# Experts' weights in loads of 1 MB with 8 KB rows, and sorted rows by one indirect gather per two experts

## The chip, the cores and the metric

The kernel runs on one core of one Trainium2 chip. The metric is the time of one execution on the device, in microseconds (us). A program of the framework gives each engine its own queue of instructions, which it works through in order: TensorE (PE; PEld is its weight load), VectorE (DVE), ScalarE (ACT), GpSimd (POOL) and SyncE (SP). SP computes nothing; it issues DMA transfers, which 16 DMA engines move. GpSimd issues the indirect transfers, whose row numbers lie in SBUF.

## The reference, cut to what matters

The model has two layers of a first network, each a mixer followed by a mixture of experts, and then two layers of a second network with a context of its own. The experts are what the change touches:

```python
def hier_moe(h, w_group, b_group, w_expert, b_expert, w1, w3, w2):   # 512 tokens, D = 1024
    ...
    g_val, g_idx = lax.top_k(g_prob, 1)                              # one of 4 groups
    ...
    e_val, e_idx = lax.top_k(jax.nn.softmax(e_logits, axis=-1), MOE_TOP_K)   # 2 of its 8 experts
    ...
    hid = jax.nn.silu(jnp.einsum('td,edf->tef', t, w1)) * jnp.einsum('td,edf->tef', t, w3)
    hid = hid * combine.astype(hid.dtype)[:, :, None]
    y = jnp.einsum('tef,efd->td', hid, w2)                           # 32 experts, width 128
```

512 tokens with two experts each are 1024 pairs of token and expert, on average 32 for each of 32 experts.

## The kernel before

`moe` (L727) runs once in each of the two layers of the first network. It normalizes the tokens, computes the router, counts the pairs of each expert and gives each pair a place so that pairs of one expert lie in consecutive rows. Eight indirect scatters (L872, four tiles of 128 tokens, two experts each) write the tokens' rows into `dxs` in HBM in that order. At the end eight indirect gathers (L1008) bring the experts' results back from `dys` in the tokens' order.

In between a loop (L961) runs over 16 pairs of experts q, and over a 17th step for one overflow block. An expert gets 64 rows (CAP); an expert with more has the rest in overflow blocks, of which the first is the 17th step and others would run in a loop of the device that is skipped when there are none. In step q:

- `fetch_rows` (L885) loads the sorted rows of the two experts of pair q + 2: two DMAs of SP, each 64 rows of 4 KB into 64 partitions of `xr`, starting at a place that SP reads from SBUF into a register. What belongs to the next expert comes along.
- `fetch` (L767) loads the weights of pair q + 2 by `load` (L762): four loads of the first layer's weights `w13` (two 128-row parts of D each, for both experts) and two of the second layer's `w2`, 512 KB each, in tiles of 4 KB in each of 128 partitions. The pool has WBUFS = 13 such tiles.
- `columns` (L894) transposes rows on TensorE (`px`), `hidden` (L908) multiplies with `w13` (`pa`), `turn` (L925) transposes the hidden values (`ph`), and `results` (L933) multiplies with `w2` (`py`) and scatters the result rows into `dys` by an indirect DMA on GpSimd, which leaves out rows that are not the expert's own: `blocks` (L1039) gives those a row number beyond 4096 in `rows`.
- `self.fill` (L980, L1817) mixes in steps of other work: projections of the context (`ctx_pair`, L1909). Each step loads 512 KB into a tile `stage` (L286), splits it into a high and a low part on ScalarE (`whi`, L278) and VectorE (`wlo`, L279), and multiplies (`mm`, L304). After two steps ScalarE writes `out` (L1361) and SP stores it into `dpc` (L1936). In layer 0 there are 0.7 such steps to a pair, in layer 1 one.

The framework orders each engine's instructions by a model of its own before the kernel runs; the order in the trace is the one that it found. SP's queue holds the weight loads, the row loads, the stage loads and the stores.

Of the kernel before, what the change touches and what calls it, by code (L numbers as in the profile page):

```python
# [104 lines left out]
def layout(inp):  # L105
# [54 lines left out]
    A["w13"] = w13.reshape(2, 16, 2, 4, 2, P, 256).transpose(0, 1, 3, 5, 2, 4, 6).reshape(2, 16, 4, P, 2, 512)  # L160
    A["w2"] = g["moe_w2"].reshape(2, 16, 2, P, D)
# [40 lines left out]
WBUFS = 13  # L202
# [51 lines left out]
class K:  # L254
# [472 lines left out]
    def moe(self, l, fills, tail=None, norm=False):  # L727
# [8 lines left out]
        with ExitStack() as es:  # L736
# [7 lines left out]
            dxs, dys = self.pdram.tile([D + C, D], FT, name=f"dxs{l}"), self.pdram.tile([D, D], FT, name=f"dys{l}")  # L744
            zero = pht.tile([P, D], FT, tag="ht", name=self.n("zero"))
            nc.gpsimd.memset(zero[0:C, :], 0.0)
            nc.sync.dma_start(dxs[D:, :], zero[0:C, :])
# [14 lines left out]
            def load(src):  # L762
                w = pq.tile([P, D], FT, tag="w", name=self.n("w"))
                nc.sync.dma_start(w.rearrange("p (a f) -> p a f", a=src.shape[1]) if len(src.shape) == 3 else w, src)
                return w

            def fetch(q):  # L767

                return ([load(I["w13"][l, q, kk].rearrange("p t f -> p (t f)")) for kk in range(4)],
                        [load(I["w2"][l, q, t]) for t in range(2)])  # L770
# [137 lines left out]
            def hidden(x, ws, n):  # L908

                pa = self.ps("a", "pa")  # L910
                m = KT // len(ws)
                for b, w in enumerate(ws):
                    for k in range(b * m, b * m + m):
                        for t in range(n):
                            c = t * 512 + (k - b * m) * 256
                            nc.tensor.matmul(pa[t * C:(t + 1) * C, :256], x[:, k, t * C:(t + 1) * C], w[:, c:c + 256],  # L916
                                             start=(k == 0), stop=(k == KT - 1))
# [15 lines left out]
            def results(w2, h, row):  # L933

                n = len(w2)
                r = slice(0, n * C)
                yr = pt.tile([P, D], FT, tag="yrow", name=self.n("yrow"), bufs=2)
                for b in range(2):
                    py = self.ps("mm", "py")
                    for t in range(n):  # L940
                        nc.tensor.matmul(py[t * C:(t + 1) * C, :], h[:, t * C:(t + 1) * C], w2[t][:, b * S:(b + 1) * S], start=True, stop=True)
# [6 lines left out]
            def slot(s):  # L948

                xr = fetch_rows([slots[0:1, 2, s]])  # L950
# [3 lines left out]
                ws = [load(I["w13"][l, ds(e[0], 1), b * 2:b * 2 + 2, :, ds(e[1], 1), :].rearrange("o a p u f -> (o p) (a u) f")) for b in range(2)]  # L954
                return xr, (ws, [load(I["w2"][l, ds(e[0], 1), ds(e[1], 1)].rearrange("o u p f -> (o u p) f"))])

            place = lambda q: [offi[0:1, 2 * q + t:2 * q + t + 1] for t in range(2)]
            xr = [fetch_rows(place(q)) for q in range(AHEAD)]
            prev, wrote, owed = None, [], 0.0
            x_ = columns(xr[0], 2)  # L960
            for q in range(17):  # L961
                if q + AHEAD < 16:
                    xr.append(fetch_rows(place(q + AHEAD)))
                    weights.append(fetch(q + AHEAD))
                elif q + AHEAD == 16:
                    a, b = slot(slice(0, 1))
                    xr.append(a)
                    weights.append(b)
# [1242 lines left out]
```

## Time and profile before

| | |
|---|---|
| time, median of three runs | 3120.87 us (3116.51 to 3122.72) |
| the profiled execution | 3123.15 us |
| its span, first to last instruction | 3121.4 us |
| mean granted TensorE clock, share of 2.4 GHz | 0.958 |
| busy share of the span: TensorE, VectorE, ScalarE, GpSimd | 92%, 61%, 40%, 15% |
| moved by DMA | 513.22 MB |
| weight loads of experts (L764) | 198 of 512 KB |
| row loads of experts (L891) | 66 of 256 KB |

A busy TensorE is not at its peak: its matmuls overlap, and at half the clock (1.2 GHz) it is as busy and half as fast. The granted clock in a stretch is given as a share of 2.4 GHz. The experts' loops lie at 334 to 546 us (layer 0) and 1174 to 1427 us (layer 1) of the span.

### The profile page before, as it was taken

How to read it: one execution, taken by the hardware profiler on the slowest of the kernel's cores; microseconds unless marked ns; L12 is line 12 of the kernel's file. 1: busy time of each engine (PE TensorE's matmuls, PEld its weight loads, DVE VectorE, ACT ScalarE, POOL GpSimd, SP SyncE). 2: the span in 40 equal slices, each digit the busy share in tenths (PEclk: the TensorE clock that was granted, in tenths of full speed). 3: DMA queues.
4: the chain of work that ended last, by engine and by line, in shares of the span. 5: the costliest groups of instructions: out<-in, count | busy, mean ns of one | idle time of the engine just before them, and what ended most of it. 6: DMA issues, size and time to landing. Idle time of an engine off the chain costs nothing.

```text
span 3121.4 us, 39028 instructions
## 1 busy us (share of the span) xinstructions
PE 2871.6 (92%) x14382; PEld 2198.0 (70%) x14382; DVE 1904.4 (61%) x3188; ACT 1258.4 (40%) x1989; POOL 470.5 (15%) x413
## 2 busy tenths in 40 slices
PE   7998877799999998778789999999999999999998
PEld 5566655677777785556677667777788776777887
DVE  7786312688889861115879954448745985453434
ACT  4444212456535452114653444334434344433434
POOL 0121000223313220001320000012111000001212
PEclk9998988899999999889999999999999999999999
DMA  8678988655542288786562222235644222222332
GB/s 302 208 249 291 338 291 303 220 156 170 162 150 64 87 292 303 267 292 201 164 211 89 64 62 86 67 96 177 201 128 147 84 66 68 78 93 76 95 95 81
DMA packets 177331, 513.22 MB, mean 164 GB/s; under 512 B 22768, under 2 KB 42864, under 8 KB 177136
## 3 DMA queue, kind: packets, MB, share of 16 engines
q1 hardware_dynamic: 167760, 485.51, 48.2%
q0 software_dynamic: 9376, 25.18, 2.2%
q8 instruction: 114, 1.87, 0.2%
q14 instruction: 81, 0.66, 0.1%
HBM read 472.98 MB, written 46.53 MB: 166 GB/s over the span
## 4 chain that ended last, share of the span: by engine, by line
PE 44%; DVE 4%; issue 1%; ACT 1%; DMA 1%; POOL 0%; DVEq 0%; ACTq 0%; POOLq 0%
PE mm L304 35%; PE po L1497 1%; PE pp L1494 1%; DVE wlo L279 1%; PE po L1420 1%; PE st L1409 1%; PE as L1710 1%; DMA stage<-in_modT_dram 1%; DVE stage L340 1%; PE as L1717 0%; PE pv L1606 0%; PE pv L1607 0%; PE pv L1605 0%; PE po L1431 0%; DVE junk L340 0%
## 5 line engine op out<-in xcount | busy, mean ns | idle before, releaser
L304 PE MATMUL mm<-hhi,whi 128*128 128x512 f32 (+1 forms) x2488 | 951.0, 383 | 61.1 <-ACT whi L278 52.7
L304 PE MATMUL mm<-hhi,wlo 128*128 128x512 f32 (+1 forms) x2488 | 931.9, 375 | 20.1 <-DVE wlo L279 19.7
L304 PE MATMUL mm<-hlo,whi 128*128 128x512 f32 (+1 forms) x2488 | 927.4, 373 | 1.5 <-POOL hlo L396 1.3
L279 DVE TENSOR_TENSOR wlo<-stage,whi 128x1024 fp32r<-128x1024 f32 (+2 forms) x477 | 547.0, 1149 | 458.6 <-issue 189.2
L278 ACT ACTIVATE whi<-stage 128x1024 fp32r<-128x1024 f32 (+2 forms) x477 | 461.3, 968 | 880.6 <-PE mm L304 586.5
L304 PEld LDWEIGHTS mm<-hhi,whi 128*128 128x128 f32 x2488 | 492.2, 198 | 157.6 <-ACT whi L278 58.5
L304 PEld LDWEIGHTS mm<-hhi,wlo 128*128 128x128 f32 x2488 | 492.0, 198 | 113.1 <-DVE wlo L279 31.8
L304 PEld LDWEIGHTS mm<-hlo,whi 128*128 128x128 f32 x2488 | 492.9, 198 | 85.1 <-issue 16.6
L340 DVE SCALAR_TENSOR_TENSOR stage<-stage,row 128x1024 f32<-128x1024 f32 x160 | 211.8, 1333 | 24.2 <-DMA stage<-in_adaT_dram 15.7
L1622 DVE SCALAR_TENSOR_TENSOR cv<-cfu,cols,cv 128x512 f32<-128x512 f32 x240 | 171.5, 756 | 1.3
L1586 POOL TENSOR_TENSOR merged<-sig,merged 128x512 f32<-128x512 f32 x48 | 83.7, 1744 | 560.2 <-DVE sig L1585 551.0
L304 PE MATMUL mm<-brh,whi 128*128 128x512 f32 (+1 forms) x384 | 142.4, 371 | 13.5 <-DVE merged L1583 5.8
L304 PE MATMUL mm<-brh,wlo 128*128 128x512 f32 (+1 forms) x384 | 141.8, 372 | 12.9 <-DVE wlo L279 12.6
L304 PE MATMUL mm<-brl,whi 128*128 128x512 f32 (+1 forms) x384 | 139.0, 362 | 0.1
L916 PE MATMUL pa<-w,xc 128*64 128x256 f32 x1056 | 126.3, 381 | 0.2 <-issue 0.2
L903 DVE COPY xc<-px 128x512 f32<-128x512 f32 (+1 forms) x34 | 23.0, 675 | 157.8 <-PE px L900 157.8
L916 PEld LDWEIGHTS pa<-w,xc 128*64 128x64 f32 x1056 | 77.7, 138 | 52.8 <-issue 17.7
L943 POOL DMA_INDIRECT dys<-yrow,ri x32 | 32.1, 1004 | 469.9 <-DVE yrow L1102 449.8
L304 PEld LDWEIGHTS mm<-brh,whi 128*128 128x128 f32 x384 | 74.6, 194 | 29.2 <-DVE merged L1583 6.6
L304 PEld LDWEIGHTS mm<-brh,wlo 128*128 128x128 f32 x384 | 74.2, 194 | 28.5 <-DVE wlo L279 16.7
L1361 ACT ACTIVATE att<-as,stat 128x512 f32<-128x512 f32 (+2 forms) x80 | 54.7, 687 | 69.6 <-DVE stat L1472 66.0
L304 PEld LDWEIGHTS mm<-brl,whi 128*128 128x128 f32 x384 | 74.9, 195 | 9.7 <-issue 0.5
(474 smaller groups left out, 4283.4 us busy)
## 6 DMA issues: line engine op xcount, KB each, us to landing
stage<-in_winA_dram SPq DMA_DIRECT2D x252, 512.0 KB
w<-in_w_dram SPq DMA_DIRECT2D x198, 512.0 KB
stage<-in_adaT_dram SPq DMA_DIRECT2D x96, 512.0 KB
stage<-in_modT_dram SPq DMA_DIRECT2D x64, 512.0 KB
stage<-in_ssmA_dram SPq DMA_DIRECT2D x49, 512.0 KB
stage<-in_wbrA_dram SPq DMA_DIRECT2D x96, 256.0 KB
xr<-dxs SPq DMA_DIRECT2D x66, 256.0 KB
stage<-in_woutA_dram SPq DMA_DIRECT2D x24, 512.0 KB
```

The lines of the kernel that those rows point to most:

```text
L278: self.nc.scalar.activation(hi, src, AF.Copy)
L279: self.nc.vector.tensor_tensor(lo, src, hi.bitcast(FT), op=OP.subtract)
L304: nc.tensor.matmul(ps[:, po:po + n], w[:, k * P:(k + 1) * P], h[:, so:so + n], start=(k == first and w is hi and h is hh), stop=(k == last ...
L340: self.nc.vector.scalar_tensor_tensor(t if out is None else out, t, 1.0, vec, op0=OP.mult, op1=OP.mult, accum_out=acc)
L916: nc.tensor.matmul(pa[t * C:(t + 1) * C, :256], x[:, k, t * C:(t + 1) * C], w[:, c:c + 256], start=(k == 0), stop=(k == KT - 1))
L943: i = nc.gpsimd.indirect_dma_start(out=dys[:, :], out_offset=bass.IndirectOffsetOnAxis(ap=row, axis=0), in_=yr[r, :], in_offset=None, boun ...
L1361: self.nc.scalar.activation(out, in_, func, **kw)
L1409: nc.tensor.matmul(q["ps"][:, i, :T], kT[:, j * P:(j + 1) * P], qT, start=True, stop=True)
L1420: nc.tensor.matmul(q["po"][:, :T], v[j][:, h * P:(h + 1) * P], q[j], start=(j == 0), stop=(j == nt - 1 and cross is None))
L1494: nc.tensor.transpose(pp[:, o:o + P], stat[hh][:, c:c + P], self.cm("ident"))
L1586: nc.gpsimd.tensor_tensor(merged[f], sg, merged[f], op=OP.add)
L1622: nc.vector.scalar_tensor_tensor(c, u[:, t:t + T], self.col(f"cfw{l}_{t}", i), c, op0=OP.mult, op1=OP.add)
```

## The change

Weights: the host lays `w13` out so that one load of 1 MB brings four 128-row parts of D for both experts, with 8 KB for each partition, and `w2` so that one load brings both experts' second layers. A pair has three loads; the pool has six tiles of 8 KB per partition in place of 13 of 4 KB. In the overflow step the two halves of `w13` go into one tile, in runs of 1 KB (2 KB before).

Rows: the two loads of SP become one indirect gather on GpSimd, with the row numbers that the scatter of results uses already; rows beyond `dxs` are left out, and what stood in the buffer stays. The first use of each of the three buffers is cleared by a memset. The block of zeros behind `dxs` and the registers with the places go.

```diff
-    A["w13"] = w13.reshape(2, 16, 2, 4, 2, P, 256).transpose(0, 1, 3, 5, 2, 4, 6).reshape(2, 16, 4, P, 2, 512)
-    A["w2"] = g["moe_w2"].reshape(2, 16, 2, P, D)
+    A["w13"] = w13.reshape(2, 16, 2, 2, 4, P, 256).transpose(0, 1, 3, 5, 4, 2, 6)
+    A["w2"] = g["moe_w2"].reshape(2, 16, 2, P, D).transpose(0, 1, 3, 2, 4)
...
-WBUFS = 13
+WBUFS = 6
...
-            dxs, dys = self.pdram.tile([D + C, D], FT, name=f"dxs{l}"), self.pdram.tile([D, D], FT, name=f"dys{l}")
-            zero = pht.tile([P, D], FT, tag="ht", name=self.n("zero"))
-            nc.gpsimd.memset(zero[0:C, :], 0.0)
-            nc.sync.dma_start(dxs[D:, :], zero[0:C, :])
+            dxs, dys = (self.pdram.tile([D, D], FT, name=f"{n}{l}") for n in ("dxs", "dys"))
...
-            def load(src):
-                w = pq.tile([P, D], FT, tag="w", name=self.n("w"))
-                nc.sync.dma_start(w.rearrange("p (a f) -> p a f", a=src.shape[1]) if len(src.shape) == 3 else w, src)
+            def load(*src):
+                w = pq.tile([P, 2 * D], FT, tag="w", name=self.n("w"))
+                for i, a in enumerate(src):
+                    n = int(np.prod(a.shape[1:]))
+                    o = w[:, i * n:(i + 1) * n]
+                    nc.sync.dma_start(o.rearrange("p (a f) -> p a f", a=a.shape[1]) if len(a.shape) == 3 else o, a)
                 return w
 
             def fetch(q):
 
-                return ([load(I["w13"][l, q, kk].rearrange("p t f -> p (t f)")) for kk in range(4)],
-                        [load(I["w2"][l, q, t]) for t in range(2)])
+                return ([load(I["w13"][l, q, h].rearrange("p k t f -> p (k t f)")) for h in range(2)],
+                        load(I["w2"][l, q].rearrange("p t f -> p (t f)")), 2)
...
-            def fetch_rows(places):
+            def fetch_rows(row, first=False):
 
                 xr = pt.tile([P, D], FT, tag="row", name=self.n("xr"), bufs=3)
-                for t, ap in enumerate(places):
-                    at = nc.values_load(ap, engines=[ET.SP], min_val=0, max_val=D,
-                                        skip_runtime_bounds_check_because="a place among 1024 pairs")
-                    nc.sync.dma_start(xr[t * C:(t + 1) * C, :], dxs[ds(at, C), :])
+                if first:
+                    nc.gpsimd.memset(xr, 0.0)
+                nc.gpsimd.indirect_dma_start(
+                    out=xr[0:row.shape[0], :], out_offset=None, in_=dxs[:, :],
+                    in_offset=bass.IndirectOffsetOnAxis(ap=row, axis=0), bounds_check=D - 1, oob_is_err=False)
                 return xr
...
             def slot(s):
 
-                xr = fetch_rows([slots[0:1, 2, s]])
...
-                ws = [load(I["w13"][l, ds(e[0], 1), b * 2:b * 2 + 2, :, ds(e[1], 1), :].rearrange("o a p u f -> (o p) (a u) f")) for b in range(2)]
-                return xr, (ws, [load(I["w2"][l, ds(e[0], 1), ds(e[1], 1)].rearrange("o u p f -> (o u p) f"))])
+                w13 = [I["w13"][l, ds(e[0], 1), h, :, :, ds(e[1], 1), :].rearrange("o p k u f -> (o p) (k u) f") for h in range(2)]
+                return [load(*w13)], load(I["w2"][l, ds(e[0], 1), :, ds(e[1], 1)].rearrange("o p u f -> (o p) (u f)")), 1
...
-            place = lambda q: [offi[0:1, 2 * q + t:2 * q + t + 1] for t in range(2)]
-            xr = [fetch_rows(place(q)) for q in range(AHEAD)]
+            rows = [rows[:, q:q + 1] for q in range(16)] + [srow[0:C, 0:1]]
+            xr = [fetch_rows(rows[q], True) for q in range(AHEAD)]
...
             for q in range(17):
-                if q + AHEAD < 16:
-                    xr.append(fetch_rows(place(q + AHEAD)))
-                    weights.append(fetch(q + AHEAD))
-                elif q + AHEAD == 16:
-                    a, b = slot(slice(0, 1))
-                    xr.append(a)
-                    weights.append(b)
+                if q + AHEAD < 17:
+                    xr.append(fetch_rows(rows[q + AHEAD], q + AHEAD < 3))
+                    weights.append(fetch(q + AHEAD) if q + AHEAD < 16 else slot(slice(0, 1)))
```

The matmuls, their number and their order in the program stay; `hidden` and `results` only find their weights at other offsets.

## Rows read from the trace of the kernel before

**Rows 1.** The page, DMA queues: packets, MB, share of 16 engines' span.
```profile
q0 software_dynamic: 9376, 25.18, 2.2%
```

**Rows 2.** Stretches: length, engines' busy us (instructions), clock, DMA share, GB/s.
```profile
348.00:416.00 68.00, 53.97 (x352) 34.22 (x350) 11.14 (x19) 12.11 (x27) 5.87 (x6) 0.87 1.03 331
422.00:546.00 124.00, 95.67 (x564) 63.30 (x565) 24.60 (x36) 25.03 (x48) 10.29 (x11) 0.85 0.88 302
1174.00:1223.00 49.00, 42.02 (x310) 29.48 (x309) 10.64 (x16) 10.78 (x22) 2.95 (x3) 0.93 0.87 300
1223.00:1390.00 167.00, 124.52 (x747) 90.05 (x747) 29.62 (x41) 31.82 (x58) 9.75 (x10) 0.82 0.81 278
```

**Rows 3.** DMA in 40 slices: 422 to 466 us (busy tenths, rate), 1256 to 1289 us.
```profile
DMA  4999998999999999999999999999999999610000
GB/s 188 210 391 376 387 328 257 313 413 417 417 425 417 421 417 428 220 220 220 369 402 421 417 425 417 417 421 387 179 231 223 298 395 406 268 75 15 0 0 0
...
GB/s 0 184 214 333 358 402 392 417 387 353 298 233 293 358 402 417 422 417 412 437 412 422 417 303 228 238 223 248 313 382 417 343 219 55 10 0 0 0 0 0
```

**Rows 4.** SP's queue from store to store in layer 1: start, us, instruction.
```profile
1256.43 0.33 SPq L1936 DMA_DIRECT2D dpc<-out  x1
1256.84 1.36 SPq L764 DMA_DIRECT2D w<-in_w_dram  x3
1258.30 0.38 SPq L286 DMA_DIRECT2D stage<-in_winA_dram  x1
1259.19 1.45 SPq L891 DMA_DIRECT2D xr<-dxs  x2
1260.73 5.17 SPq L764 DMA_DIRECT2D w<-in_w_dram  x6
1267.13 0.33 SPq L286 DMA_DIRECT2D stage<-in_winA_dram  x1
1268.03 1.99 SPq L891 DMA_DIRECT2D xr<-dxs  x2
1270.83 2.79 SPq L764 DMA_DIRECT2D w<-in_w_dram  x3
1288.64 0.33 SPq L1936 DMA_DIRECT2D dpc<-out  x1
```

**Rows 5.** SP's waits, 334 to 546 us, then 1174 to 1427: us, times, longest.
```profile
SPq L764 <- DMA w<-in_w_dram: 44.7, 45, 2.3
SPq L1936 <- ACT out L1361: 40.4, 3, 14.4
...
SPq L1936 <- ACT out L1361: 85.8, 7, 15.1
SPq L764 <- DMA w<-in_w_dram: 20.5, 24, 2.3
```

**Rows 6.** TensorE's waits, 334 to 546 us, then 1174 to 1427.
```profile
PE px L900 <- DMA xr<-dxs: 12.6, 6, 3.4
...
PE mm L304 <- ACT whi L278: 34.7, 13, 5.1
```

**Rows 7.** Timelines of ScalarE and TensorE, same cycle: start, us, [idle before, releaser].
```profile
1265.53 1.06 ACT L278 ACTIVATE whi<-stage 128x1024 fp32r<-128x1024 f32 x1 [1.39 <-DMA stage<-in_winA_dram]
...
1266.64 0.43 PE L304 MATMUL mm<-hhi,whi 128*128 128x256 f32 x1 [2.87 <-ACT whi L278]
1272.76 1.48 PE L900 MATMUL px<-cmt,xr 128*128 128x128 f32 x8
1282.34 0.39 PE L304 MATMUL mm<-hhi,whi 128*128 128x256 f32 x1 [1.37 <-ACT whi L278]
```

**Rows 8.** GpSimd: result scatters of layer 1 (ns min/median/max), landing, a memset.
```profile
L943 POOL DMA_INDIRECT dys<-yrow,ri x16: 975/976/1375, 1192.9 to 1420.3; - x16
DMA to landing us min/median/max: 6.8/8.7/9.1
...
L746 POOL MEMSET zero<- 64x1024 f32 x2 | 1.9, 946 | 22.6 <-PE po L667 22.6
```

More of the change, by code (lines that the diff above doesn't have):

```diff
@@ L910, in hidden @@
                 pa = self.ps("a", "pa")
[L911 to L917, printed above, removed]
+                for k in range(KT):
+                    for t in range(n):
+                        c = (k * n + t) * 256
+                        w = ws[c // (2 * D)]
+                        c %= 2 * D
+                        nc.tensor.matmul(pa[t * C:(t + 1) * C, :256], x[:, k, t * C:(t + 1) * C], w[:, c:c + 256],
+                                         start=(k == 0), stop=(k == KT - 1))
                 r = slice(0, n * C)
@@ L931, in turn, with results @@
                 return h
-            def results(w2, h, row):
-                n = len(w2)
+            def results(w2, h, row, n):
                 r = slice(0, n * C)
@@ L940, in results @@
                     for t in range(n):
-                        nc.tensor.matmul(py[t * C:(t + 1) * C, :], h[:, t * C:(t + 1) * C], w2[t][:, b * S:(b + 1) * S], start=True, stop=True)
+                        nc.tensor.matmul(py[t * C:(t + 1) * C, :], h[:, t * C:(t + 1) * C], w2[:, t * D + b * S:t * D + (b + 1) * S], start=True, stop=True)
                     self.halves(b, yr[r, :], py[r, :])
@@ L961, in moe @@
             for q in range(17):
-                if q + AHEAD < 16:
-                    xr.append(fetch_rows(place(q + AHEAD)))
-                    weights.append(fetch(q + AHEAD))
-                elif q + AHEAD == 16:
-                    a, b = slot(slice(0, 1))
-                    xr.append(a)
-                    weights.append(b)
-                ws, w2 = weights[q]
-                x, n = x_, len(w2)
+                if q + AHEAD < 17:
+                    xr.append(fetch_rows(rows[q + AHEAD], q + AHEAD < 3))
+                    weights.append(fetch(q + AHEAD) if q + AHEAD < 16 else slot(slice(0, 1)))
+                ws, w2, n = weights[q]
+                x = x_
                 if q < 16:
-                    x_ = columns(xr[q + 1], len(weights[q + 1][1]) if q < 15 else 1)
+                    x_ = columns(xr[q + 1], weights[q + 1][2])
                 if prev:
@@ L976, in moe @@
                 if prev:
-                    wrote.append(results(prev[0], hd, prev[2]))
+                    wrote.append(results(prev[0], hd, *prev[2:]))
                 for _ in range(2):
@@ L982, in moe @@
                 owed -= int(owed)
-                prev = w2, hd_, rows[:, q:q + 1] if q < 16 else srow[0:C, 0:1]
-            wrote.append(results(prev[0], turn(prev[1], 1), prev[2]))
+                prev = w2, hd_, rows[q], n
+            wrote.append(results(w2, turn(hd_, n), *prev[2:]))
             for i, a in enumerate(wrote):
@@ L992, in moe @@
                 with tc.For_i(1, SLOTS, 1) as s:
-                    xr, (ws, w2) = slot(ds(s, 1))
-                    hd = hidden(columns(xr, 1), ws, 1)
+                    ws, w2, n = slot(ds(s, 1))
                     row = pt.tile([P, 1], I32, tag="rowi", name=self.n("rowi"), bufs=1)
                     nc.vector.tensor_copy(row, srow[:, ds(s, 1)])
-                    results(w2, turn(hd, 1), row[0:C, :])
+                    hd = hidden(columns(fetch_rows(row[0:C, :]), n), ws, n)
+                    results(w2, turn(hd, n), row[0:C, :], n)
             self.fill(fills["rows"])
```

## The prediction, made before the changed kernel ran

> **What bounds the kernel now.** I read the page first, then the stretches in which experts run, then one cycle of SP's queue in each of them. The edit touches only the two passes through the experts: 334 to 546 us (loop 0) and 1174 to 1427 us (loop 1). Windows over these show two regimes [rows 2]. From 348 to 416 us the DMA engines are busy throughout (share 1.03, 331 GB/s) and TensorE's granted clock is 0.87: bytes set the pace. From 422 to 546 and from 1223 to 1390 us the share is 0.88 and 0.81 and the clock 0.85 and 0.82: neither TensorE nor the DMA is full.
>
> The slices of DMA rate show why [rows 3]. While 512 KB weight loads stream, slices read 412 to 437 GB/s. There are three kinds of holes: slices at 220 GB/s, slices around 179 to 248, and, at the end of each stretch, zeros. The 220s are the sorted rows: two loads of 64 partitions each. The zeros are SP's own doing. SP issues in order, and a store of context results (L1936) stands in its queue and waits for ScalarE's `out`: 40.4 us in three waits in loop 0, 85.8 us in seven in loop 1 [rows 5]. All loads behind it wait too, and the DMA runs dry.
>
> So in loop 1 the cycle of two pairs is a chain, not a throughput: from store to store 1288.64 - 1256.43 = 32.2 us [rows 4]. Its links: the store at 1256.43, three weight loads, then stage load S1 at 1258.30; ScalarE begins to split S1 at 1265.53, having waited for its landing; TensorE stood idle for 2.87 us before S1's first matmul at 1266.64, is done at 1272.76, does a pair, and begins S2's matmuls at 1282.34 [rows 7]; then the next store. Sorted rows are in none of these links (they are issued behind S1). In loop 0 a cycle has three pairs, and there S1 stands behind one pair of row loads; TensorE also waited 12.6 us in six places for rows directly, against 34.7 us for a split in loop 1 [rows 6].
>
> **The change part by part.**
>
> *Rows.* Per pair, two SP loads of 256 KB go and one gather on GpSimd's queue comes. Old price: 0.524 MB at 220 GB/s = 2.4 us of DMA [rows 3]. The gather drops rows out of bounds. That such rows move no bytes is seen in the software queue: 25.18 MB [rows 1], less 16 scatters and 16 gathers of 128 full rows (32 x 0.524 = 16.8 MB), leaves 8.4 MB for the result scatters with the same index columns, which is 2048 rows of 4 KB for two layers, 64 a pair and not 128. So the gather moves 0.262 MB. No gather inside the loops is in the trace; by bounds it costs 0.262/0.42 = 0.6 us at the streaming rate or 0.262/0.22 = 1.2 us at the half rate. I take 0.9, the middle, since both rates occur with scatters beside them. Saving: 1.5 us of DMA a pair (1.2 to 1.8).
>
> What of it lies on the path: in the saturated start of loop 0, SP issues about eight pairs' rows before 402 us, but the first pairs are paced by TensorE. I count five whole savings, 7.5 us, and 2.5 us of the half clock that follows TensorE's waits for rows (0.87 in this stretch): -10 us (-5 to -14). Loop 1's saturated start (1174 to 1223, share 0.87) holds one or two such pairs: -2 us (0 to -4). In loop 0's later cycles one pair of rows stands before S1: -1.5 us in each of three, -4.5 us. In loop 1's five steady cycles: nothing, the DMA only runs dry earlier.
>
> GpSimd's side: a scatter takes 0.976 us of its time and lands after 8.7 us [rows 8]; a gather as long, issued a pair or more ahead (three row buffers), is covered, because GpSimd is busy for 2.95 us of 49 [rows 2] and nothing but the scatters queues behind it. If that cover were gone, px would wait as it does for rows now. Three memsets of 128x1024 before the first gathers: 0.946 us each by the 64-partition one [rows 8], on an idle engine, nothing. The zero block's memset and store go: nothing, they ran long before. SP loses 66 row loads with their register reads; it is not short of issue time where the DMA is full.
>
> *Weights.* Six loads of 512 KB become three of 1 MB. Slices already read up to 437 GB/s with 4 KB rows and mostly 412 to 425 [rows 3], so the rate gains between 0 and about 4%, 0.3 us of 7.5 us a pair: I take 0. SP's waits of 44.7 us in 45 pieces for earlier weight loads [rows 5] are back-pressure of a full DMA, and only become fewer and longer. The overflow block's halves now have 1 KB runs: between 0 and 1 us each layer, two pairs ahead of use; 0.
>
> The Trainium skill speaks for more here. "SBUF — State Buffer", section "The DMA setup-cost knee", says each transfer carries about 2 us that does not scale with bytes and advises the largest single transfer. 96 loads fewer would by that be 190 us (an estimate from the page). The slices at 412 to 437 GB/s with 512 KB loads show that queued transfers hide it; only a load after a dry queue pays it.
>
> *Buffers.* 13 of 4 KB become six of 8 KB. This decides what SP can issue before it meets the store. In the trace it is 3 + 3: three weight loads (1.57 MB) before the store, three after it, ahead of S1 ([rows 4] is one of nine such places). In whole MB loads it must be 1 + 2 or 2 + 1, so S1 is behind 2.1 or 1.05 MB in place of 1.57: +-0.52 MB / 0.42 = +-1.25 us a cycle. Counting buffers (two second-layer tiles and the current pair's three are still held: five of six) speaks for 1 + 2; the instruction order is made anew for the changed program, which speaks for neither. I take half of the worse, +0.6 us in each of five cycles of loop 1 and three of loop 0: +5 us (-10 to +10).
>
> Sum: -10 - 2 - 4.5 + 5 = -11.5, say -12 us. The profiled execution took 3123.15 us (span 3121.4) and so would take 3111; the median of the runs is 2.3 us lower, 3120.87, which gives 3109 us. Its own range, from the bounds above: -4.5 is held, -10 goes from -5 to -14, -2 from 0 to -4, +5 from -10 to +10, taken together some 3092 to 3121.
>
> **The rivals.**
> 1. *S1 behind the whole pair (slower).* If the store lands ahead of all three 1 MB loads in SP's queue, S1 waits behind 3.15 MB: 1.57/0.42 = +3.75 us a cycle, five in loop 1 and three in loop 0, +30 us; with the rows' -16.5 that is +14, 3135 us. It decides as soon as more than about 2.1 MB stand between store and S1. For it: six coarse buffers, of which one may be late. Against: three of six loads came before the store each time.
> 2. *The clock comes back (faster).* TensorE ran at 0.82 to 0.87 of 2.4 GHz in these stretches, that is about a third of the time at 1.2 GHz, each time after an idle stretch such as the 2.87 us [rows 2, 7]. S1's matmuls took 6.1 us (1266.64 to 1272.76). If S1 lands 2 us sooner and the idle goes, a cycle loses those 2 us and about 3 us of half clock: 5 us x 8 cycles = 40, with the start 52: 3070 us. For it: 2 + 1 would suffice. Against: S2 pays its own 1.37 us idle by ScalarE's order, which nothing here changes.
> 3. *Hidden anyway.* Both loops wait for S1 and the store, and the start's gain is given back at the first store of loop 0 (the queue ran dry before 422 us already). Time 3121. For it: the zeros in the slices.
> 4. *The change doesn't do what it says.* If the gather moved all 128 rows, it would cost 0.524/0.42 = 1.2 us, a saving of 1.2 for 1.5: 3112 us. Against: the 8.4 MB.
> 5. *A fixed price for each load.* SP's waits for earlier weight loads are 65 us in both loops (44.7 in loop 0, 20.5 in loop 1 [rows 5]). Were they the price of single loads, half would go: -33 - 12, 3076 us. The skill's knee would mean that; the 412 to 437 GB/s speak against it.
>
> **How the numbers follow.** Forecast 0.45; rival 1 0.20; rival 2 0.15; rival 3 0.13; rival 4 0.04; rival 5 0.03. A measurement of this kernel tells about 0.2% (6.2 us) from no change: faster means under 3114.6, slower over 3127.1. Of the forecast's 0.45 about 0.36 lies below 3114.6; with rivals 2 and 5 and half of 4: 0.56 faster. Rival 3, the rest of the forecast and of 4: 0.24 same. Rival 1: 0.20 slower. The range must leave out 0.2: 3070 (rival 2 at its centre) to 3135 (rival 1 at its centre) leaves out about half of each; I set 3070 to 3136.
>
> **What would show it.** In the changed profile: no 220 GB/s slices apart from those beside scatters; no px wait for rows; the software queue at 25.2 + 8.4 = 33.6 MB (42 if rival 4 holds); SP's queue in loop 1 with one or two weight loads between store and S1 (three: rival 1); the distance store to store in loop 1 at 31 to 34 us (36 for rival 1, 27 for rival 2); loop 0 from its first px to its last scatter shorter by 10 to 15 us; streaming slices still at about 420 GB/s (rival 5 would show no change there but fewer gaps). I would be wrong above all if the order on SP or TensorE comes out otherwise than in the trace of before, since the later cycles hang on where S1 and the store stand.

## The result, and the profile after

The changed kernel takes 3012.49 us (median of four runs, 3008.18 to 3013.05) beside 3121.8 us for the kernel before on the same chip (3116.51 to 3126.65): a ratio of 0.9647, 95% interval 0.9629 to 0.9665. That is 109 us less; the forecast was 12 us less, and its range went down to 3070. The profiled execution took 3013.05 us, its span 3011.3 us.

All of the gain lies in the two loops. Layer 0's loop begins at 335 us in the kernel before and at 337 in the changed one; its last scatter (`sr`) now starts at 503.0 us instead of 545.9: 43 us. Layer 1's last scatter starts at 1318.0 instead of 1427.1: 109 us, so 66 more. What follows takes 1693 us in the new kernel and 1694 in the old.

Windows over the two loops, kernel before, then after (columns as in [rows 2]):

```profile
334.00:546.00 212.00, 168.28 (x1048) 111.10 (x1047) 40.72 (x64) 42.98 (x84) 16.17 (x17) 0.86 0.91 305
1174.00:1427.00 253.00, 198.37 (x1253) 142.60 (x1252) 51.27 (x70) 54.00 (x97) 16.03 (x16) 0.85 0.82 280
```
```profile
335.00:504.00 169.00, 151.11 (x1073) 96.51 (x1072) 40.55 (x66) 41.87 (x85) 35.60 (x34) 0.98 0.92 362
1130.00:1319.00 189.00, 174.45 (x1256) 118.11 (x1255) 50.04 (x70) 51.45 (x96) 34.06 (x31) 1.00 0.91 349
```

Two things stand out: the clock granted to TensorE, 0.86 and 0.85 before, is 0.98 and 1.00 of 2.4 GHz, and the DMA moves 349 to 362 GB/s instead of 280 to 305. GpSimd is busy twice as long; TensorE waited for its gathers once, 2.5 us (below).

SP's queue from store to store in layer 1, after (answers to [rows 4]):

```profile
1240.77 0.33 SPq L1931 DMA_DIRECT2D dpc<-out  x1
1241.19 0.38 SPq L286 DMA_DIRECT2D stage<-in_winA_dram  x1
1241.66 1.36 SPq L764 DMA_DIRECT2D w<-in_w_dram  x3
1243.11 0.39 SPq L286 DMA_DIRECT2D stage<-in_winA_dram  x1
1243.60 4.16 SPq L764 DMA_DIRECT2D w<-in_w_dram  x3
1264.95 0.33 SPq L1931 DMA_DIRECT2D dpc<-out  x1
```

This is one part of the result. Before, the store stood in the middle of a pair's loads, with three loads between it and S1. Now S1 stands straight behind the store, all loads of the pair that TensorE is working on stand ahead of it, and a cycle of the same two pairs takes 24.2 us instead of 32.2. In the first half of each loop there is not even that: the stage loads went ahead of the weights, and 33 loads of 1 MB in loop 0 (21 in loop 1) stream with nothing between them but a store to every six to nine.

The other part is TensorE's own order. Its instructions in that cycle (answers to [rows 7]; from `ph` to S1's first matmul, the first with the low part, the pair behind the fill):

```profile
1244.70 0.33 PE L929 MATMUL ph<-cmt,hd 128*128 128x128 f32 x1 [0.99 <-DVE hd L923]
1245.45 1.94 PE L941 MATMUL py<-w,hT 128*64 128x512 f32 x8 [0.43 <-ACT hT L931]
1247.32 0.65 PE L901 MATMUL px<-cmt,xr 128*128 128x128 f32 x4
1248.22 0.38 PE L304 MATMUL mm<-hhi,whi 128*128 128x256 f32 x1 [0.25 <-ACT whi L278]
...
1249.48 0.38 PE L304 MATMUL mm<-hhi,wlo 128*128 128x256 f32 x1 [0.32 <-DVE wlo L279]
...
1252.30 1.08 PE L917 MATMUL pa<-w,xc 128*64 128x256 f32 x7
```

The wait ahead of S1's matmuls is 0.25 us (2.87 before), and from the first to the end they take 4.1 us (6.1). In the kernel before TensorE worked in the order `px`, `py`, `pa`, `ph`, fill. The fill's matmuls stood directly behind `ph`, and ScalarE began their split only behind `hT`, which needs `ph`; so TensorE waited 1.37 us ahead of S2's matmuls [rows 7] behind this line, although ScalarE did not wait for S2 to land:

```profile
1280.64 0.33 PE L928 MATMUL ph<-cmt,hd 128*128 128x128 f32 x1 [0.70 <-DVE hd L922]
```

Now `py` and `px` stand between `ph` and the fill, and the split is made meanwhile. TensorE's waits for split weights and SP's longest waits in layer 1's loop, after (answers to [rows 5, 6]):

```profile
PE mm L304 <- DVE wlo L279: 2.8, 6, 0.8
PE mm L304 <- ACT whi L278: 1.9, 3, 0.8
```
```profile
SPq L1931 <- ACT out L1356: 66.9, 5, 17.3
SPq L764 <- PE pa L917: 48.4, 21, 5.5
```

TensorE waited 1.9 us for split high parts where it had waited 34.7. SP still stands 66.9 us at the store (85.8 before), but by then both pairs are on their way. The DMA from 400 to 440 us, in 40 slices, where [rows 3] had 220 and zeros:

```profile
GB/s 434 424 414 426 434 408 422 420 426 426 426 418 422 418 361 393 422 418 422 426 418 434 410 373 311 303 410 426 367 330 373 402 397 432 377 365 418 428 422 418
```

And the rows' new price: the software queue ([rows 1] had 25.18 MB), the gathers, the memsets of their buffers, and what TensorE waited for them.

```profile
q0 software_dynamic: 14144, 33.58, 3.1%
...
L890 POOL DMA_INDIRECT xr<-dxs,ri x32: 984/1014/1702, 331.1 to 1226.2; - x32
L889 POOL MEMSET xr<- x6: 952/954/977, 325.0 to 1120.1; 128x1024 f32 x6
...
  PE px L901: 2.5, 1
```

### The profile page after: what moved, and what is told of

Its sections match the earlier page's. It is cut to its first block, busy times and chain, and to the rows that moved or that the text cites. A ratio compares the mean times of both kernels' runs of the same rounds, so it can differ in the third digit from the quotient of the medians.

```text
span 3011.3 us, 38668 instructions
## 1 busy us (share of the span) xinstructions
PE 2827.6 (94%) x14382; PEld 2157.5 (72%) x14382; DVE 1902.1 (63%) x3188; ACT 1254.9 (42%) x1989; POOL 512.4 (17%) x451
## 3 DMA queue, kind: packets, MB, share of 16 engines
q0 software_dynamic: 14144, 33.58, 3.1%
## 4 chain that ended last, share of the span: by engine, by line
PE 45%; DVE 4%; issue 1%; ACT 1%; DMA 1%; POOL 0%; DVEq 0%; ACTq 0%; POOLq 0%
PE mm L304 36%; PE po L1492 1%; PE pp L1489 1%; DVE wlo L279 1%; PE po L1415 1%; PE st L1404 1%; PE as L1705 1%; DVE stage L340 1%; PE as L1712 1%; DMA stage<-in_modT_dram 1%; PE pv L1602 0%; PE pv L1601 0%; DVE junk L340 0%; PE po L1426 0%; PE pv L1600 0%
## 5 line engine op out<-in xcount | busy, mean ns | idle before, releaser
L304 PE MATMUL mm<-hhi,whi 128*128 128x512 f32 (+1 forms) x2488 | 932.8, 375 | 11.9 <-ACT hhi L391 4.3
L304 PE MATMUL mm<-hhi,wlo 128*128 128x512 f32 (+1 forms) x2488 | 912.7, 367 | 16.6 <-DVE wlo L279 16.3
L304 PE MATMUL mm<-hlo,whi 128*128 128x512 f32 (+1 forms) x2488 | 909.8, 366 | 0.7 <-POOL hlo L396 0.7
L304 PEld LDWEIGHTS mm<-hhi,whi 128*128 128x128 f32 x2488 | 474.6, 191 | 113.3 <-issue 27.5
L304 PEld LDWEIGHTS mm<-hhi,wlo 128*128 128x128 f32 x2488 | 474.2, 191 | 106.0 <-DVE wlo L279 24.3
L304 PEld LDWEIGHTS mm<-hlo,whi 128*128 128x128 f32 x2488 | 474.6, 191 | 84.9 <-issue 17.6
L340 DVE SCALAR_TENSOR_TENSOR stage<-stage,row 128x1024 f32<-128x1024 f32 x160 | 210.8, 1327 | 24.3 <-DMA stage<-in_adaT_dram 16.6
L304 PE MATMUL mm<-brh,wlo 128*128 128x512 f32 (+1 forms) x384 | 142.3, 374 | 12.7 <-DVE wlo L279 12.4
L917 PE MATMUL pa<-w,xc 128*64 128x256 f32 x1056 | 132.4, 391 | 4.1 <-DMA w<-in_w_dram 4.0
L304 PEld LDWEIGHTS mm<-brh,wlo 128*128 128x128 f32 x384 | 75.2, 197 | 27.8 <-DVE wlo L279 16.1
L353 POOL TENSOR_TENSOR sqa<-sq,sqa 128x512 f32<-128x512 f32 (+1 forms) x44 | 58.5, 1329 | 188.8 <-ACT sq L355 183.5
L1196 POOL TENSOR_TENSOR aL<-cmt,aah 128x512 fp32r<-128x512 f32 x32 | 51.1, 1598 | 171.1 <-PE pe L1198 143.4
```

The source lines that it names most:

```text
L304: nc.tensor.matmul(ps[:, po:po + n], w[:, k * P:(k + 1) * P], h[:, so:so + n], start=(k == first and w is hi and h is hh), stop=(k == last ...
L340: self.nc.vector.scalar_tensor_tensor(t if out is None else out, t, 1.0, vec, op0=OP.mult, op1=OP.mult, accum_out=acc)
L353: (engine or nc.gpsimd).tensor_tensor(self.sq_acc, self.sq_last, self.sq_acc, op=OP.add)
L1196: nc.gpsimd.tensor_tensor(aL, self.cm("le")[:, None, :].to_broadcast([P, 4, P]), part[:, c, hsl, None].bitcast(FT).to_broadcast([P, 4, P]) ...
```

## The experiments

Ratios are to the kernel before on the same chip, with 95% intervals; "loop 0 ends" and "loop 1 ends" are the starts of the two `sr` scatters.

| kernel | median, us | ratio | interval | loop 0 ends | loop 1 ends |
|---|---|---|---|---|---|
| before | 3121.8 | 1 | | 545.9 | 1427.1 |
| after | 3012.5 | 0.9647 | 0.9629-0.9665 | 503.0 | 1318.0 |
| e1 rows alone | 3020.2 | 0.9673 | 0.9644-0.9701 | 504.9 | 1329.4 |
| e2 weights alone | 3110.9 | 0.9972 | 0.9952-0.9992 | 544.0 | 1416.3 |
| e3 after, stage loads held | 3029.5 | 0.9701 | 0.9672-0.9731 | 508.4 | 1335.7 |
| e4 before, stage loads early | 3090.7 | 0.9897 | 0.9866-0.9929 | 548.5 | 1398.1 |
| e5 before, rows on GpSimd | 3060.4 | 0.9811 | 0.9794-0.9829 | 525.5 | 1372.1 |
| e6 after, all rows gathered | 3022.5 | 0.9695 | 0.9677-0.9714 | 505.2 | 1326.7 |
| e7 after, two loads behind the store | 3113.6 | 0.9971 | 0.9954-0.9988 | 541.4 | 1420.8 |
| e8 after, stage loads early | 3004.4 | 0.9635 | 0.9611-0.9659 | 506.0 | 1306.3 |
| e9 after, halves | 3027.1 | 0.9700 | 0.9679-0.9722 | 503.7 | 1328.7 |
| e10 before, store by ScalarE | 3101.6 | 0.9934 | 0.9910-0.9959 | 539.0 | 1402.8 |
| e11 after, store by ScalarE | 3018.9 | 0.9661 | 0.9632-0.9689 | 507.6 | 1324.2 |
| e12 after, e8 and e11 | 2998.1 | 0.9607 | 0.9582-0.9631 | 505.3 | 1301.9 |
| e13 after, one load behind the store | 3054.8 | 0.9773 | 0.9744-0.9801 | 520.2 | 1364.0 |
| e14 after, three behind the store | 3127.5 | 1.0008 | 0.9992-1.0024 | 546.9 | 1435.0 |

The theory at first (A): once the row loads have left SP's queue, the order is made anew, and it is that order, above all the stage loads' lead over the weights, that pays. Its rivals were the rows' bytes and half rate (B) and the size of the loads (C); theory D (order and rows' DMA time, both) came after the first four runs.

**e1, rows alone.** The kernel before, with the change's `fetch_rows` and nothing of its loads.

> The rows' part of the change alone: sorted rows by one gather of GpSimd, weights still in loads of 512 KB in 13 tiles of 4 KB. Theory A (order): with the row loads gone from SP's queue the order of SP's instructions is made anew, the fill's stage loads come ahead of the experts' weights, TensorE is no longer short of split weights and its clock stays at 2.4 GHz. A expects most of the 109 us: 3010 to 3035 us, granted clock of loop 0 and loop 1 at 0.95 or more. Rival B (bytes: the half-rate row loads and other experts' rows are the cause, whatever the order) expects the same here, 3010 to 3040. Rival C (the size of the weight loads is the cause) expects little: 3095 to 3120.

0.9673: nearly the whole gain, so it isn't the size of the loads. A and B both stand.

**e2, weights alone.** The kernel before, with the change's `load`, `fetch` and WBUFS = 6.

> The weights' part alone: loads of 1 MB in six tiles of 8 KB, rows still by two loads of SP for a pair. In SP's queue the stage loads stand between the pairs' weights as in the kernel before, and the store stands behind two of the three loads of a pair. A and B expect little: 3095 to 3130 us, clock in the loops at 0.82 to 0.88. C expects most of the gain: 3010 to 3040.

0.9972, little, as A and B had it. It came out in the prediction's 2 + 1 order (two loads, the store, one load, S1), and its cycles in layer 1 are 31.1 us in the mean (four from 1252.62 us on), 1.7 less than before (32.8, five from 1223.75 us on), where the prediction had 1.25 for that case.

**e3, stage loads held.** The changed kernel; a stage load of the loop may not be ahead of the weight loads that the program issued before it.

```diff
+        i = self.nc.sync.dma_start(t[:, :width], src)
+        if self.held is not None:
+            self.tc.add_manual_dep(i.ins, self.held.ins.name, mybir.DependencyInfo(mybir.DependencyClass.NoSync, mybir.DependencyReason.DATA), reason="in the program's order")
...
                     weights.append(fetch(q + AHEAD) if q + AHEAD < 16 else slot(slice(0, 1)))
+                    self.held = self.last
```

> The changed kernel, bytes and load sizes as they are, but each stage load of a fill is held behind the weight loads that the program issued before it, as in the kernel before: SP's queue reads stage, three weight loads, stage, three weight loads, store. A expects most of the gain to go: 3060 to 3110 us, TensorE again waiting for split weights for 25 us or more in the two loops and the clock there under 0.93. B and C expect the gain to stay: 3010 to 3030.

A missed: 0.9701, about 17 us lost and not 50 to 100, with the clock at 1.00 in both loops. So the stage loads' lead over the weights is a small part. But this order leaves the store in its new place. SP's queue in layer 1 reads

```profile
1236.54 0.33 SPq L1936 DMA_DIRECT2D dpc<-out  x1
1236.95 0.38 SPq L287 DMA_DIRECT2D stage<-in_winA_dram  x1
1237.43 1.35 SPq L767 DMA_DIRECT2D w<-in_w_dram  x3
1238.88 0.39 SPq L287 DMA_DIRECT2D stage<-in_winA_dram  x1
1239.36 4.17 SPq L767 DMA_DIRECT2D w<-in_w_dram  x3
1260.75 0.33 SPq L1936 DMA_DIRECT2D dpc<-out  x1
```

a cycle of 24.2 us as in the changed kernel: S1 is straight behind the store and no pair is cut in two by it. In layer 0 of e3 all three loads of a pair stand between the store and S1, and the clock there is 1.00 too; so it is not S1's place alone that counts.

**e4, stage loads early in the kernel before.** `proj` keeps its next three stage tiles asked for; `src` is the list of what is still to load and of the tiles at hand.

```diff
+            todo, have = src
+            while todo and len(have) < 4:
+                have.append(self.stage(todo.pop(0)))
+            t = have.pop(0)
```

> The kernel before, rows and weights loaded as they were (bytes unchanged, half-rate row loads on SP), but the program asks for a fill's stage tiles three steps ahead, so that a split weight doesn't wait behind a pair's loads. A expects a large part of the gain with no byte less: 3035 to 3075 us, TensorE's waits for the split high part under 10 us in each loop, clock in the loops over 0.92. B and C expect 3100 to 3125.

0.9897, three tenths of the gain, between what A and what B and C gave. The wait at the store has shrunk (12.7 us in loop 1 for 85.8), and in a middle stretch of layer 1 the DMA is full but slow:

```profile
1201.69:1262.10 60.41, 48.92 (x327) 34.50 (x323) 12.85 (x18) 12.73 (x24) 3.90 (x4) 0.89 1.03 333
```

333 GB/s at a share of 1.03: with the order mended, the rows' half rate would be the bound. This reading made theory D. A's other signs failed: TensorE still waited 19.8 us for split high parts in layer 1's loop, though ScalarE waited only 4.9 us for stage tiles, and the clock was 0.88. That wait lies in the two engines' own order (see e10).

**e5, rows on GpSimd.** The kernel before; the two row loads of a pair, byte for byte, are issued by GpSimd.

```diff
-                    at = nc.values_load(ap, engines=[ET.SP], min_val=0, max_val=D,
-                    nc.sync.dma_start(xr[t * C:(t + 1) * C, :], dxs[ds(at, C), :])
+                    at = nc.values_load(ap, engines=[ET.Pool], min_val=0, max_val=D,
+                    nc.gpsimd.dma_start(xr[t * C:(t + 1) * C, :], dxs[ds(at, C), :])
```

> The kernel before with its two row loads for a pair as they were (64 rows of 4 KB to 64 partitions each, other experts' rows included), but issued by GpSimd in place of SP. SP's queue then comes out as with the rows' part of the change: the stage loads ahead, 17 to 18 weight loads between stores. Theory A (order alone): 3015 to 3040 us, as with the gather. Theory D (both: with the order mended the loops are bound by the DMA, and the row loads' 2.4 us a pair at half rate count in full): 3060 to 3095, DMA share in the loops over 0.94. Rival B (bytes and rate alone, the order doesn't matter): 3100 to 3125.

0.9811, at the edge of D's range: 59 us from leaving SP's queue, at the old bytes and half rate. Both orders came out new: SP's, as expected, and TensorE's, with `py` and `px` between `ph` and the fill. The remaining 43 us to e1 are the price of the rows' transfers. The streaming stretch of layer 1 (three stores' worth, six pairs) in e5, then in e1:

```profile
1176.02:1244.16 68.14, 62.47 (x460) 41.57 (x458) 14.57 (x22) 14.40 (x31) 12.76 (x19) 0.95 1.03 352
```
```profile
1153.93:1210.13 56.20, 56.20 (x440) 39.97 (x438) 14.58 (x22) 14.36 (x30) 12.20 (x12) 1.00 1.02 403
```

Both at a full DMA, 352 against 403 GB/s, 12 us for six pairs. In e1 TensorE is busy throughout as well, so 403 need not be all that the DMA gives.

**e6, all rows gathered.** The changed kernel with an index that leaves out nothing: other experts' rows come along as they did before.

```diff
+            nc.vector.tensor_scalar(self.every[r, :], pair(off, t), row[r, :], float(D - 1), op0=OP.add, op1=OP.min)
...
-                    xr.append(fetch_rows(rows[q + AHEAD], q + AHEAD < 3))
+                    xr.append(fetch_rows(every[q + AHEAD], q + AHEAD < 3))
```

> The changed kernel with a gather that reads all 128 rows of a pair, other experts' rows included (0.262 MB more a pair, 33 pairs and blocks: 8.4 MB, 42 MB in the software queue). Theory A: the order stays and TensorE sets the pace: 3010 to 3018 us. Theory D: 0.6 us more of DMA a pair, up to 20 us where the DMA is full: 3015 to 3033. Rival B: bytes are the cause, so half the gain or more goes: over 3050.

0.9695, with 42.01 MB in the software queue: 8.4 MB cost about 15 us. Of the rows' 43 us that is a third. The rest fits the half rate of 64 partitions, but no run separates that from what else differs between e5 and e1 (two loads or one, direct or by row numbers).

**e7, e13, e14, the store between a pair's loads.** The changed kernel in the orders that the prediction had assumed: e3's rule, and the last two (e7), one (e13) or all three (e14) loads of a pair may not be ahead of the store (`self.stored`; `self.pair` counts the pair's loads, and the bound of 0 is 1 in e13 and gone in e14).

```diff
+                    if self.stored is not None and self.pair > 0:
+                        self.tc.add_manual_dep(self.last.ins, self.stored.ins.name, mybir.DependencyInfo(mybir.DependencyClass.NoSync, mybir.DependencyReason.DATA), reason="the store first")
+                    self.pair += 1
```

> The changed kernel with the order that the prediction assumed: in each cycle the store stands behind one weight load of a pair, the pair's other two loads (2.1 MB) stand between the store and S1, three loads between S1 and S2. Bytes and load sizes stay. The prediction's own sum for this order: about 3117 us in the 1 + 2 case, cycles of 32 to 34 us in layer 1. Theories A and D (the place of S1 behind the store makes the chain): 3070 to 3120 us, clock in layer 1's loop under 0.93. Rival B (rows' bytes and rate are all): 3025 to 3040.

> The changed kernel in the order of the run with two loads behind the store, but with only one of a pair's three loads (1.05 MB) between the store and the stage load. Even steps from 3029 us (none behind) to 3113.6 us (two behind): 3065 to 3078 us. A threshold (one load is covered by the five tiles ahead of it): 3029 to 3045 us. The prediction put this order at 1.25 us a cycle less than the old one, 3095 to 3105 us.

> The changed kernel with all three loads of a pair (3.15 MB) between the store and the stage load, the first rival of the prediction, which put it at 3135 us. Even steps of 42 us a load: 3145 to 3165 us. The chain grows by the transfer time alone (1.05 MB at 420 GB/s, 2.5 us, in some 12 cycles: 30 us): 3135 to 3150 us.

The bytes, the gather and the 1 MB loads are all there, and the gain is gone: 0.9971 in e7, 1.0008 in e14. SP's queue of e7:

```profile
1257.59 0.33 SPq L1941 DMA_DIRECT2D dpc<-out  x1
1258.00 1.70 SPq L768 DMA_DIRECT2D w<-in_w_dram  x2
1259.76 0.42 SPq L288 DMA_DIRECT2D stage<-in_winA_dram  x1
1260.27 1.92 SPq L768 DMA_DIRECT2D w<-in_w_dram  x3
1262.29 0.39 SPq L288 DMA_DIRECT2D stage<-in_winA_dram  x1
1262.78 0.46 SPq L768 DMA_DIRECT2D w<-in_w_dram  x1
1289.98 0.33 SPq L1941 DMA_DIRECT2D dpc<-out  x1
```

Cycles of 24.3 (none, e3), 26.4 (one), 31.2 (two) and 32.8 us (three), means of six in layer 1, stand against 3029, 3055, 3114 and 3128 us. The steps are 25, 59 and 14 us: neither even nor one threshold. e13 lies in none of its three ranges, 40 us under the one from the prediction, and e14 lies under both of its own. Nor is it S1 that TensorE waits for here. Its longest wait in layer 1's loop, in e7 and in e14:

```profile
PE pa L924 <- DMA w<-in_w_dram: 23.7, 7, 4.8
```
```profile
PE pa L924 <- DMA w<-in_w_dram: 39.7, 8, 6.3
```

It is the pair's own loads behind the store that come too late for `pa`. What counts is how far the loads are ahead when SP stands at the store: at layer 1's second store TensorE has done 5.25 pairs of `pa`, and SP has issued the loads of 6.00 pairs in e3, 5.67 in e13 and 5.33 in e7; in e14 both are 5.00. In e13 the one load behind is `w2`, which is needed last, and TensorE's wait for it is 8.9 us; that `w2` is the cheap step and `w13` the dear one fits the uneven steps, but no run changed the loads' order to show it.

e13 also answers e2. In layer 1's cycles the two have the same order of store, stage loads and weight loads on SP's queue (one load, S1, three, S2, two, store); only e2's row loads stand between. e13 is 62 us faster (0.9773 against 0.9972), with cycles of 26.4 us for 31.1. So with store and S1 in the same places, the rows' part of the change is worth 62 us. In the traces, what differs most is what TensorE waits for in layer 1's loop, in e2 and in e13:

```profile
PE mm L304 <- ACT whi L278: 26.3, 12, 4.0
```
```profile
PE mm L308 <- ACT whi L280: 2.6, 4, 1.3
```

e2 has TensorE's old order and e13 the new one. No run divides the 62 us between that order and the rows' transfers.

**e9, halves.** The changed kernel; each tile is filled by two loads of 512 KB.

> The changed kernel, each 8 KB tile filled by two loads of 512 KB with 4 KB rows (6 loads a pair as before, bytes as in the changed kernel; SP's order of stage loads, weights and stores stays within one load). A and D: the size of a load costs nothing: 3008 to 3020 us. Rival C (each load has a fixed price, 96 loads or about 33 us by the prediction's fifth rival): 3035 to 3050.

0.9700, between the two expectations: up to 16 us. The loops themselves show about 9: from its first weight load on, loop 0 is 4 us longer (it ends 0.7 us later and begins 3.6 earlier) and loop 1 is 5 (it ends 10.7 us later and begins 5.9 later).

**e8, e10, e11, e12, what is left.** The stage loads early, as in e4, in the changed kernel (e8); the store issued by ScalarE in the kernel before (e10) and in the changed kernel (e11); e8 and e11 together (e12).

```diff
-            nc.sync.dma_start(self.dpc[i], o.rearrange("p j t -> p (j t)"))
+            nc.scalar.dma_start(self.dpc[i], o.rearrange("p j t -> p (j t)"))
```

> The changed kernel, in which the program asks for a fill's stage tiles three steps ahead in both loops. A and D: TensorE hardly waits for split weights any more in the changed kernel (2.7 us in both loops), so little is left to gain: 2998 to 3012 us. If SP's blocking behind the store (66.9 us in layer 1's loop) still costs time: 2975 to 2998.

> The kernel before, only the store of the context's results is issued by ScalarE, which computes them, in place of SP: nothing in SP's queue waits for ScalarE any more, rows and weights as before. Theory D: the chain through the store goes, and the loops are bound by DMA with half-rate rows, as when stage tiles are asked for ahead: 3060 to 3095 us, DMA share over 0.94 in both loops. If the store had no part in the chain: 3110 to 3125.

> The changed kernel with the store issued by ScalarE. SP's 83 us behind the store in the two loops go. If they still cost time: 2985 to 3005 us, store-to-store distances of 20 to 22 us for 24 in the later half of layer 1's loop. If TensorE sets the pace by now: 3005 to 3015.

> Both on the changed kernel: stage tiles asked for three steps ahead, and the store issued by ScalarE. Either alone should take most of what is left; together 2985 to 3004 us. If ScalarE's issuing delays its splits: above 3010.

In the kernel before, taking the store out of SP's queue gives 0.9934 and no more, between the two expectations. TensorE still waits 16.1 us for split high parts in loop 1 (34.7 before), but not because loads are late: from 1254 to 1375 us neither ScalarE nor a matmul waits for any load. TensorE's order there is the old one, and the waits are its own:

```profile
1269.23 0.33 PE L928 MATMUL ph<-cmt,hd 128*128 128x128 f32 x1 [0.70 <-DVE hd L922]
1270.87 0.38 PE L304 MATMUL mm<-hhi,whi 128*128 128x256 f32 x1 [1.31 <-ACT whi L278]
...
1276.35 1.04 PE L900 MATMUL px<-cmt,xr 128*128 128x128 f32 x8
1277.69 1.94 PE L941 MATMUL py<-w,hT 128*64 128x512 f32 x8 [0.30 <-ACT xc L905]
1279.45 3.62 PE L916 MATMUL pa<-w,xc 128*64 128x256 f32 x32
```
```profile
1254.00:1375.00 121.00, 95.79 (x589) 69.51 (x590) 23.82 (x33) 24.82 (x46) 7.80 (x8) 0.84 0.92 316
```

Two pairs take 29.8 us in this stretch, between the 32.8 of the kernel before and the 24.1 of the changed one (mean of its last three cycles). As an estimate from these three, some 3 us of a cycle were late loads, and the other 5.7 go with TensorE's old order and the clock of 0.84 under it. In the changed kernel the store costs nothing by itself (e11, 0.9661, a little over both its ranges): the 66.9 us that SP stands at it are not on the path. The stage loads early alone (e8, 0.9635) stay within the changed kernel's interval. With both, e12 ends layer 1's loop 16 us earlier than the changed kernel, at the full clock:

```profile
1130.00:1302.00 172.00, 165.72 (x1218) 113.21 (x1215) 46.42 (x67) 47.88 (x92) 29.78 (x30) 1.00 0.94 373
```

TensorE is busy for 166 of 172 us; there it is the bound. The changed kernel and e12 were run again:

> The changed kernel itself, on the chip of these runs: 3008 to 3015 us, a ratio of 0.963 to 0.967 to the kernel before.

> The changed kernel with stage tiles asked for three steps ahead and the store issued by ScalarE, beside the changed kernel on the same chip: ratio to the kernel before 0.958 to 0.963, at least 0.3% under that of the changed kernel, if the place of stage loads and store still costs time there; the same within 0.2% if not.

> The changed kernel itself on the same chip: ratio to the kernel before 0.963 to 0.967.

After: 0.9652 (0.9624 to 0.9680) and 0.9643 (0.9619 to 0.9666). e12's kernel: 0.9607 (0.9584 to 0.9630), 3002.6 against 3015.0 us on the same chip. It is the fastest of all, by 0.4%, with intervals that overlap a little in the last comparison.

## Why the prediction was wrong, point by point

**The step that failed** is that the orders of before were taken as given, but for the split of one pair's loads. On SP's queue: "In whole MB loads it must be 1 + 2 or 2 + 1, so S1 is behind 2.1 or 1.05 MB". It was neither: in layer 1's later cycles S1 is behind nothing. On the computing engines: "S2 pays its own 1.37 us idle by ScalarE's order, which nothing here changes". It changed: `py` and `px` now stand between `ph` and the fill, and that idle is gone. The prediction wrote that the order is made anew and that this "speaks for neither". It costed the row loads that leave SP's queue by their DMA time and by SP's issuing, and never as instructions around which everything else was placed; so it put the rows in layer 1's steady cycles at "nothing", and these cycles lost 8.7 us each (32.8 to 24.1).

What the runs show of it: the same row loads on another queue, byte for byte, bring both new orders and 59 us (e5). SP's order is needed: with cheap rows and TensorE's new order, but two loads behind the store, the gain is gone (e7). With TensorE's old order a cycle takes 29.8 us even where no load is late (e10). How the 109 us divide between the two orders is not shown, since no run has one new and the other old at the same rows. Why the framework's model places the store behind whole pairs (in e1 and e5 behind all but one load of 512 KB) and `py` ahead of the fill was not settled; the orders show only that it does.

**For one of the assumed orders the sum came out, by luck.** e7 is the 1 + 2 case: the sum gives -16.5 for the rows and +10 for the place of S1, 3116.7 us against the profiled execution and 3114 against the median; e7 took 3113.6. But TensorE waited there 23.7 us for weights and 5.4 us for split high parts, where the sum had S1's landing. For the 2 + 1 case the same terms give 3094 us, and e13, which has that order, took 3054.8. So an order that the prediction allowed would have left it 40 us short as well. What it had right is the place of S1 at the old rows: e2, the 2 + 1 case without the rows, should have been some 10 us faster than before and is 9 (0.9972). What it had wrong is the rows at 16.5 us: e2 to e13 is 62. (Its own range adds up to -32.5 us at the lower end, 3088 and not 3092.)

The terms so depend on each other: the rows' part is worth 62 us where one load stands behind the store (e2 to e13), and the whole change 9 us where two do (e7); the rows' transfers alone are worth 43 us in the new orders (e5 to e1), leaving SP's queue 59 us at the old transfers, and SP's order about 100 at the new ones (e7 to after).

**Rows, the price.** 1.5 us a pair was predicted (1.2 to 1.8); 43 us over 34 gathers are 1.3 us. The point of rival 4, 0.3 us a pair for other experts' rows, was low: e6 gives 15 us over the 32 gathers that it widens, 0.5. That dropped rows move no bytes was right to the digit: 33.58 MB for 33.6. What failed is the share of the saving that lies on the path (16.5 of some 50 us).

For the half rate the Trainium skill has a rule ("SBUF — State Buffer", section "Can I just issue two DMAs to hit both halves?"): two transfers to the two halves of the partitions don't add up, only one over 128 partitions does. The 220 GB/s of [rows 3] for the two row loads and the 352 against 403 GB/s of e5 and e1, which differ in more than this, agree.

**GpSimd's side** was right but for one wait: `px` waited once for rows, 2.5 us; the gathers take 1.01 us of GpSimd, the memsets 0.95.

**Weights, size.** 0 was predicted; e9 puts 512 KB against 1 MB at up to 16 us of 3012, and e1 against after at 8 with overlapping intervals. Streaming slices did not rise (404 GB/s mean from 400 to 440 us). Rival 5's 33 us did not come. The 190 us that the Trainium skill ("SBUF — State Buffer", section "The DMA setup-cost knee") would give for 96 loads did not show either. Such a price shows only behind an empty queue: in the changed kernel's cycle above, S1 (0.52 MB) lands 3.6 us after its issue, and the 1 MB loads queued behind it land 2.5 us apart.

**Rival 1** (S1 behind the whole pair, 3135 us) didn't happen, but e14 built it: 3127.5 us, 1.0008. Its price was right within 8 us. Its mechanism was not: `pa` waits for the weights, not the split for S1.

**Rival 2** (the clock comes back, 3070 us, 0.15) is what happened, in its own terms (idle that goes, and half clock that goes with it) and at twice its size. That 2 + 1 would suffice holds too: e13 took 3054.8. It gave a cycle 2 us of idle and 3 us of half clock; measured, the cycle lost 8.0 us. [rows 7] have idle of 2.87 and 1.37 us ahead of the two fills' matmuls; after, 0.25 ahead of S1's and none ahead of S2's. S2's idle, which the prediction held fixed, went too. And the gain was not eight cycles but the whole of both loops, from 0.86 to 0.98 of the clock in layer 0 and from 0.85 to 1.00 in layer 1.

**What would show it.** Right: no 220 GB/s in the streaming part (lowest slice 303), one short `px` wait where none was expected, 33.6 MB, streaming at 404 GB/s in the mean. Wrong: weight loads between store and S1 (none, where one or two were expected), store to store 24.2 us for 31 to 34, loop 0 from its first `px` to its last scatter shorter by 45 us for 10 to 15. The last sentence named the order on SP or TensorE as the thing that would make it wrong above all; it gave that no price and, but for rivals 1 and 2, no chance.

## What to carry to other kernels

Where the order of instructions is made by a planner, taking instructions off one queue is a change of the order on every queue and not only of their cost: before pricing the terms, ask what stood where because of them, on the DMA queue and on the computing engines, and give "the order comes out otherwise" its own time and its own chance. A store that waits in an in-order DMA queue is harmless when all loads of the unit that is needed next stand before it (e3, 24.3 us a cycle) and costs up to 8.5 us a cycle when they stand behind it (e14, 32.8), even where it cuts no unit in two. Look on the computing engine, too, for work that can stand between a step and the next one that waits for its result: in e10 loads were on time, and the cycle was still 29.8 us. And an order and a transfer's price hide each other: mending orders at the old rows gave 20 to 59 us (e10, e4, e5), the whole change in e7's order 9 us, both 109.

## What was not expected of the hardware

With no wait longer than 1.0 us, TensorE was granted 1.00 of 2.4 GHz through the whole of layer 1's loop in the changed kernel, busy for 174 of 189 us. In e7, with single waits of up to 4.8 us, it was 0.90 over the loop, and in e4, with waits of up to 3.3 us, 0.88. Long single waits are not needed for it: in e10 from 1254 to 1375 us no wait was over 1.31 us, but three (0.70, 1.31 and up to 0.76 us) stood around the start of each fill, and the clock was 0.84. A wait so costs itself and then the slower matmuls behind it: in the cycle of [rows 4] the two fills took 12.0 us from their first matmul to their last (1266.64 to 1272.97 and 1282.34 to 1287.98), in the cycle after 8.9 (1248.22 to 1252.37 and 1259.58 to 1264.30), although there other steps lie between their matmuls for 2.3 us.

The prices of the loads behind the store were not even (25, 59 and 14 us for the first, second and third); a single price for each MB, as in the prediction (about 20 us a load), comes near the first of them only.
